# A hybrid decoder layer: the first chunk transposed from raw rows, its 1/rms multiplied into the results, four loads and orders moved

## Chip, core and metric

The kernel runs on one core of a Trainium2 chip. The metric is device time in microseconds (us) of one execution. Engines: TensorE (PE; its weight loads are listed as PEld), VectorE (DVE), ScalarE (ACT), GpSimd (POOL) and SyncE (SP), whose queue issues the DMAs. The kernel before took 1467.82 us, median of three runs (1467.02 to 1468.22).

## What is computed

One layer on x (2048 tokens of 1024), all in float32:

```
hn = rms_norm(x, g_pre);  proj = hn @ w_in            # 1024 -> 4096 columns
rg_x, rg_g, da_q, da_k, da_v, da_g, xa_q, xa_g = split(proj)
A: causal depthwise conv (4) -> RG-LRU scan, times silu(rg_g)
B: (softmax(Q1 K1') - lam softmax(Q2 K2')) V, causal, 4 heads; rms_norm; times silu(da_g)
C: cross attention of 4 heads into rms_norm(mem) @ w_mem_kv (256 tokens), times silu(xa_g)
out = x + rms_norm(concat(A, B, C) @ w_out, g_post)
```

rms_norm(x, g) multiplies each token's row by 1/rms of that row and each column by g. Since 1/rms is one number per token, it may be multiplied before the projection or into its results.

## The kernel before

Every float32 operand is split in a high part (rounded to the matmul's format, on ScalarE) and a low part (the rest, on VectorE or GpSimd); a product is three matmuls, high-high, low-high, high-low (`mm3`, L241).

Tokens go in four chunks of 512, input columns in eight blocks of 128. The projection runs in two passes, chunks 0 and 1, then 2 and 3 (`project`, L847). A pass goes through 16 pairs of column blocks; each pair has four tiles (first and second half for each chunk) of 24 matmuls. Raw weight pieces (128x512) are loaded with three buffers (`w_load`, L321) and converted (`w_conv`, L327), which also issues the load of the piece three further on and later stores the converted piece to DRAM for the second pass. Each finished tile is evicted by a function of its kind: queries and keys, values, gates, cross attention, recurrence (`ev_*`, L472 to L612). Queries, keys, values and gates go through DRAM to the attention.

The order on TensorE is written out by the program: generators (`spawn`, `pump`) yield a time to wait in a modelled clock `now`, which each matmul advances, and the attention's score stream (`s_stream`, L698), its transposes and values (`t_stream`), cross attention and the recurrence's gates (`rg_gates`, L614) are woven between the projection's matmuls so. `room["e"]` counts free buffers for exponentials. The other engines and SP's queue run in order too; their order is made by a scheduler from the program's order, readiness and the priorities in the code.

The head (L370 to L382): one weight piece and the eight half rows of chunk 0 are loaded, tile after tile (a tile is 128 tokens), then weights 1 and 2, chunk 1's rows, and the memory rows. `norm_row` makes 1/rms of a row tile and multiplies its two halves by it in place. `woven` (L384) then transposes the first chunk by TensorE, block by block and two blocks ahead, evicts it with g as scale (`transpose_norm`, L293), and runs the first pair's matmuls for it. The order of the first eight tiles is pair 0 and pair 1 on chunk 0, then both on chunk 1, whose rows are normalised by `norm_steps` (L277) and transposed in the same woven way. Memory's keys and values follow.

At the end of the second pass `load_wout` (L960) loads and converts w_out's rows by groups, and the output projection runs over 16 token tiles.

Of the kernel before, what the change touches and what calls it, by code (L numbers as in the profile page):

```python
# [15 lines left out]
D = 1024  # L16
# [41 lines left out]
def hybrid_layer(  # L58
# [65 lines left out]
    ident = const.tile([128, 128], F32, name="ident")  # L124
    ones_r = const.tile([128, 128], F32R, name="ones_r")
    cmask = const.tile([128, 128], F32, name="cmask")
# [15 lines left out]
    def setup():  # L142

        nc.scalar.preload_act_table_set("natural_log_exp_and_others")
        nc.scalar.dma_start(vec, vecs[:, 0:V_CW])
        make_identity(nc, ident)
        nc.gpsimd.memset(cmask, 0.0)
        nc.gpsimd.affine_select(
            out=cmask, in_=cmask, pattern=[[-1, 128]], compare_op=ALU.is_ge,
            fill=NEG, base=0, channel_multiplier=1)  # L150
        nc.vector.memset(epsb, EPS)
        nc.vector.memset(tinyb, 1e-37)
        nc.vector.tensor_scalar(ones_r, ident, 0.0, 1.0, op0=ALU.mult, op1=ALU.add)

# [108 lines left out]

    def norm_row(row):

        ss = tiny.tile([128, 2], F32, tag="ss1", name="ss1")
        ja, jv = f2("junk", (128, 512)), f2("junk", (128, 512))
        nc.scalar.activation(ja, row[0], AF.Square, accum_out=ss[:, 0:1])
        nc.vector.tensor_tensor_reduce(jv, row[1], row[1], 1.0, 0.0, ALU.mult, ALU.add, ss[:, 1:2])
        r = tiny.tile([128, 1], F32, tag="rs1", name="rs1")  # L270
        with tc.high_priority(offset=2000):
            nc.vector.tensor_add(r, ss[:, 0:1], ss[:, 1:2])
            rsqrt_mean(r, r, D, nc.vector)
            for p in row:
                nc.vector.tensor_scalar_mul(p, p, r)

# [91 lines left out]
    ready = set()  # L368
    stored = set()
    setup()  # L370
    w_load(0)
    xr0 = load_rows(x, 4, "xrow")
    w_load(1, 2)
    xb = bigt("xrows", (128, 4, 2, 512), F32)
    xr1 = [[xb[:, i, j, :] for j in range(2)] for i in range(4)]
    for i in range(4):
        nc.sync.dma_start(xb[:, i].rearrange("p a b -> p (a b)"), x[CH + i * 128:CH + (i + 1) * 128, :])
    mrows = load_rows(mem, 2, "memx")
    w_conv(0)
    for row in xr0:  # L380
        norm_row(row)
    w_conv(1, 2, eng=nc.vector)  # L382

    def woven(c, rows):  # L384

        new_hnT(c)
        os = [ps_m("ip") for _ in range(2)]
        xt = transpose_norm(rows, hnT[c], V_GPRE)
        next(xt)
        next(xt)  # L390
        for kb in range(KB):
            w = wcv[kb // 2]
            for half in range(2):
                cs = slice(half * 128, half * 128 + 128)
                mm3(os[half], w[:, 0, kb % 2, cs], w[:, 1, kb % 2, cs], hnT[c][0][:, kb, :], hnT[c][1][:, kb, :],
                    kb == 0, kb == KB - 1)
            next(xt, None)
            if c == 0:
                if kb in (1, 2, 4, 6):
                    i = {1: 3, 2: 4, 4: 5, 6: 6}[kb]  # L400
                    w_conv(i, eng=nc.vector if i in (3, 5) else nc.gpsimd, pool=pw if i < 6 else p4)
            elif kb % 2:
                w_conv(MEM0 + kb // 2, eng=nc.vector if kb % 4 == 1 else nc.gpsimd)
            pump()
        if c == 0:
            w_conv(7, pool=p4)
        ready.add(c)
        return os

    def prep_mem():  # L410
# [59 lines left out]


    def ev_qk(h, c, which, o):  # L472
        t = f4("qkhl", (128, 2, CH), F32R)
        if which == 0:
            nc.scalar.activation(t[:, 0], o, AF.Copy, scale=DA_SCALE)
            nc.vector.scalar_tensor_tensor(t[:, 1], o, DA_SCALE, asf(t[:, 0]), op0=ALU.mult, op1=ALU.subtract)
        else:
            nc.scalar.copy(t[:, 0], o)
            nc.vector.tensor_sub(t[:, 1], o, asf(t[:, 0]))

        def st():
            for k in range(2):
                rows = asf(t[k * 64:(k + 1) * 64])
                dst = (QD, KD)[which][h][c][k]
                nc.sync.dma_start(dst[0:2].rearrange("l r t -> r l t"), rows)
                if which == 0:
                    nc.sync.dma_start(dst[2], rows[:, 0, :])
        store(st, 3.0)

    def ev_v(hp, c, half, o):  # L490

        t = f4("vhl", (128, 2, 2, 2, 128), F32R)
        ov = o.rearrange("p (t h d) -> p h t d", t=2, h=2)
        for hh in range(2):
            nc.scalar.copy(t[:, 0, hh], ov[:, hh])
            nc.vector.tensor_sub(t[:, 1, hh], ov[:, hh], asf(t[:, 0, hh]))
        def st():
            for hh in range(2):
                nc.sync.dma_start(VD[2 * hp + hh][c][:, :, 2 * half:2 * half + 2, :], asf(t[:, :, hh]))
        store(st, 3.0)  # L500

    def ev_g(hp, c, half, o):
        t = f2("gs", (128, CH))
        sigmoid(t, o)
# [12 lines left out]

    def ev_xa(h, c, which, o):
        if which == 0:
            sg = f2("xag", (128, CH))  # L520
# [62 lines left out]
    def ev_rg(b, c, which, o):  # L583
        if which == 0:
# [5 lines left out]
            else:  # L590
                nc.gpsimd.tensor_copy(xr[:, 0:3], halo[:, b, :])
            nc.scalar.copy(xr[:, 3:515], o)
            if c < NCH - 1:
# [12 lines left out]
            return  # L606
        xc, xh = state.pop("xc")
        gs = f2("rgg", (128, CH))
        sigmoid(gs, o)
# [4 lines left out]
    def rg_gates(b, c, xc, xh, gs):  # L614
        while state["xa_live"]:
            yield 0.5
        if "rgh" not in state:
            rg_weights()
            yield 5.0
        ri = f4("ri", (128, 2, CH))  # L620
        for g in range(2):
            o = ps_s("rgo")
            mm3(o, state["rgh"][:, b, g, :], state["rgl"][:, b, g, :], xh[:, 0], xh[:, 1], True, True)
            with tc.high_priority(offset=PRX):
# [73 lines left out]
    def s_stream(jobs):  # L698

        q2s = {}  # L700

        def q2_load(i):
            if i < 2 * len(jobs) and i not in q2s:
                h, pr = jobs[i // 2]
                if has("qk", h, pr // 4):
                    q2s[i] = load_q2(h, 2 * pr + i % 2)
        due = now[0]
        for ij, (h, pr) in enumerate(jobs):
            while 2 * ij not in q2s:
                q2_load(2 * ij)  # L710
                yield 0.5
            while kready.get((h, pr // 4), 1e9) > now[0]:
                yield 0.5
# [118 lines left out]
    def subln(h, pr, A, B):  # L832
        c, j = divmod(pr, 2)
        s = ps_t("ss", (128, 256))
        mm(s, ones_r, B[:, 0, :], True, False)
        mm(s, ones_r, B[:, 1, :], False, True)
        r = A[:, 1, :]
# [71 lines left out]
    def start_attention():  # L909
        room["e"] = N_E  # L910
        spawn(kv_stream())
# [20 lines left out]
    def prep_next(c):  # L932
        yield from prep_x(c, xn.pop(c), False)
        if c == 2:
            room["e"] += 8
        else:
            room["kv"] += 1
# [20 lines left out]


    def load_wout(grp):  # L960

# [5 lines left out]
        for kb in range(4):  # L967
            raw = f4("woraw")
            nc.sync.dma_start(raw, w_out[4 * grp + kb])
            for j in range(2):  # L970
# [7 lines left out]

    project((2, 3), 80, ORDER_B, {(0, 0): start_b, (15, 2): last_pair})

# [117 lines left out]
```

## Time and profile before

| | |
|---|---|
| median of three runs | 1467.82 us |
| profiled execution | 1467.53 us, its span 1465.7 us |
| TensorE busy | 1412.3 us, 96% of the span |
| VectorE, ScalarE, GpSimd busy | 61%, 53%, 33% |
| mean granted TensorE clock | 0.994 |

The span goes from the first to the last instruction of one profiled execution. Busy time is the union of an engine's instructions; matmuls overlap, so the time from one start to the next is the better measure of one matmul. A wait is the idle time of an engine before an instruction, put down to what released it.

### The profile page before, as it was taken

How to read it: one execution, taken by the hardware profiler on the slowest of the kernel's cores; microseconds unless marked ns; L12 is line 12 of the kernel's file. 1: busy time of each engine (PE TensorE's matmuls, PEld its weight loads, DVE VectorE, ACT ScalarE, POOL GpSimd, SP SyncE). 2: the span in 40 equal slices, each digit the busy share in tenths (PEclk: the TensorE clock that was granted, in tenths of full speed). 3: DMA queues.
4: the chain of work that ended last, by engine and by line, in shares of the span. 5: the costliest groups of instructions: out<-in, count | busy, mean ns of one | idle time of the engine just before them, and what ended most of it. 6: DMA issues, size and time to landing. Idle time of an engine off the chain costs nothing.

```text
span 1465.7 us, 21854 instructions
## 1 busy us (share of the span) xinstructions
PE 1412.3 (96%) x7568; PEld 1199.2 (82%) x7568; DVE 898.3 (61%) x1872; ACT 775.9 (53%) x1900; POOL 477.3 (33%) x568
## 2 busy tenths in 40 slices
PE   5999999999999899999999999999999999999997
PEld 3798889888887678888887898888877888888886
DVE  6531555676644876746547666757678777767222
ACT  6343544666547784745555545555566545554221
POOL 2031333344435632412213222212255333334221
PEclk9999999999999999999999999999999999999999
DMA  8689787745433348356324554232475334322231
GB/s 298 180 263 338 230 240 237 247 143 181 166 119 110 134 163 247 121 173 196 114 97 118 165 177 168 86 113 70 143 251 169 101 135 150 102 76 94 87 122 72
DMA packets 147870, 234.37 MB, mean 160 GB/s; under 512 B 12464, under 2 KB 82224, under 8 KB 147760
## 3 DMA queue, kind: packets, MB, share of 16 engines
q1 hardware_dynamic: 147616, 232.98, 48.8%
q8 instruction: 59, 0.97, 0.3%
q14 instruction: 51, 0.42, 0.1%
q10 hardware_dynamic: 144, 0.01, 0.0%
HBM read 142.76 MB, written 90.18 MB: 159 GB/s over the span
## 4 chain that ended last, share of the span: by engine, by line
PE 73%; DVE 9%; ACT 7%; DMA 4%; POOL 3%; issue 3%; SPq 1%; DVEq 0%; POOLq 0%; ACTq 0%
PE ip L198 36%; PE po L198 16%; PE s L198 7%; PE o L198 6%; PE pt L202 3%; PE xas L198 2%; DVE e L766 1%; DVE nm L740 1%; PE xao L198 1%; DMA q<-QD 1%; DVE xc L600 1%; PE rgo L198 1%; ACT e L742 1%; PE xat L202 1%; POOL e L765 1%
## 5 line engine op out<-in xcount | busy, mean ns | idle before, releaser
L198 PE MATMUL ip<-hnT,wp 128*128 128x512 f32 x2688 | 680.5, 397 | 6.9 <-DVE rgg L610 2.6
L198 PEld LDWEIGHTS ip<-hnT,wp 128*128 128x128 f32 x2688 | 496.0, 190 | 109.8 <-DVE hnT L307 4.5
L742 ACT ACTIVATE e<-s,nm 128x512 f32<-128x512 f32 (+3 forms) x320 | 200.1, 626 | 254.7 <-DVE nm L740 235.8
L740 DVE TENSOR_REDUCE nm<-s 128x1 f32<-128x512 f32 (+3 forms) x320 | 193.4, 605 | 37.4 <-PE s L198 33.1
L198 PE MATMUL po<-wout,yg 128*128 128x512 f32 x768 | 193.4, 393 | 5.0 <-POOL wout L239 2.4
L765 POOL TENSOR_SCALAR e<-e,f 128x512 f32<-128x512 f32 (+3 forms) x160 | 121.3, 773 | 235.5 <-DVE f L761 161.6
L198 PE MATMUL s<-kv,q 128*128 128x512 f32 (+3 forms) x640 | 182.9, 367 | 3.9 <-DMA q<-QD 2.4
L198 PEld LDWEIGHTS po<-wout,yg 128*128 128x128 f32 x768 | 141.1, 188 | 35.4 <-POOL wout L239 4.2
L766 DVE SCALAR_TENSOR_TENSOR e<-e,f 128x512 f32<-128x512 f32 (+3 forms) x160 | 138.0, 887 | 29.9 <-POOL e L765 29.7
L807 DVE TENSOR_TENSOR pthl<-pt,pthl 128x512 fp32r<-128x512 f32 (+1 forms) x144 | 94.5, 656 | 68.0 <-ACT pthl L806 67.5
L198 PE MATMUL o<-pthl,kv 128*128 128x256 f32 (+1 forms) x864 | 134.3, 290 | 1.0 <-DVE pthl L807 0.9
L198 PEld LDWEIGHTS s<-kv,q 128*128 128x128 f32 x640 | 114.5, 189 | 25.1 <-DMA q<-QD 3.0
L239 POOL TENSOR_TENSOR wp<-wraw,wp 128x512 fp32r<-128x512 f32 x67 | 91.1, 1368 | 127.1 <-ACT wp L238 110.8
L198 PEld LDWEIGHTS o<-pthl,kv 128*128 128x128 f32 x864 | 114.1, 189 | 4.5 <-DVE pthl L807 1.8
L806 ACT CAST pthl<-pt 128x512 fp32r<-128x512 f32 (+1 forms) x144 | 80.7, 561 | 55.2 <-PE pt L202 54.5
L239 POOL TENSOR_TENSOR yg<-yraw,yg 128x512 fp32r<-128x512 f32 x48 | 64.2, 1341 | 132.8 <-ACT yg L238 122.4
L198 PE MATMUL ip<-wp,hnT 128*128 128x256 f32 x768 | 99.7, 284 | 1.3 <-POOL wp L239 0.8
L198 PEld LDWEIGHTS ip<-wp,hnT 128*128 128x128 f32 x768 | 95.8, 191 | 3.0 <-POOL wp L239 1.0
L198 PE MATMUL po<-wo,yg 128*128 128x512 f32 x384 | 97.2, 392 | 0.0
L202 PE MATMUL pt<-ident,e 128*128 128x128 f32 x544 | 83.0, 272 | 3.3 <-DVE pthl L807 3.3
L198 PEld LDWEIGHTS po<-wo,yg 128*128 128x128 f32 x384 | 71.0, 188 | 14.3
L202 PEld LDWEIGHTS pt<-ident,e 128*128 128x128 f32 x544 | 66.9, 140 | 18.4 <-DVE pthl L807 3.8
(188 smaller groups left out, 1686.1 us busy)
## 6 DMA issues: line engine op xcount, KB each, us to landing
WD<-wp SPq DMA_DIRECT2D x64, 512.0 KB, 4.7
wp<-WD SPq DMA_DIRECT2D x64, 512.0 KB, 4.3
wraw<-in_w_in_dram SPq DMA_DIRECT2D x64, 256.0 KB, 3.4
q<-QD SPq DMA_DIRECT2D x128, 128.0 KB, 3.7
kv<-KD SPq DMA_DIRECT2D x24, 512.0 KB, 5.9
kv<-VD SPq DMA_DIRECT2D x24, 512.0 KB, 6.2
yraw<-YD SPq DMA_DIRECT2D x48, 256.0 KB, 2.7
QD<-qkhl SPq DMA_DIRECT2D x32, 256.0 KB, 3.5
```

The costliest lines, as they stand in the source:

```text
L198: nc.tensor.matmul(o, w, xx, start=start, stop=stop)
L202: nc.tensor.transpose(o, i, ident)
L239: eng.tensor_sub(lo, raw, asf(hi))
L600: nc.vector.scalar_tensor_tensor(xc[:, 0:CH], xr[:, k:k + CH], vec2[:, cw + k:cw + k + 1], xc[:, 0:CH], op0=ALU.mult, op1=ALU.add)
L740: nc.vector.tensor_reduce(out=nm[:, c, kc:kc + 1], in_=s[:, 0:w], op=ALU.max, axis=AX.X, negate=True)
L742: nc.scalar.activation(e[kc, c][:, 0:w], s[:, 0:w], AF.Exp, bias=nm[:, c, kc:kc + 1], accum_out=l[:, c, kc:kc + 1])
L765: nc.gpsimd.tensor_scalar(e2, e2, f[:, 1, kc:kc + 1], 1.0, op0=ALU.mult, op1=ALU.mult)
L766: nc.vector.scalar_tensor_tensor(e1, e1, f[:, 0, kc:kc + 1], e2, op0=ALU.mult, op1=ALU.add)
L806: nc.scalar.copy(hi[:, 0:n], t[:, 0:n])
L807: nc.vector.tensor_sub(lo[:, 0:n], t[:, 0:n], asf(hi[:, 0:n]))
```

## The change

The first chunk's rows are loaded left halves first, with weights 1 and 2 between and after. They are transposed unnormalised; 1/rms is computed beside the projection (`inv_rms`), laid out along the free axis for all partitions by four TensorE transposes (`spread`, into rB0, which takes one of the twelve buffers for exponentials), and multiplied into the evictions of chunk 0. The second chunk's and memory's loads move into and behind `woven`. The first conversion is by VectorE, the next seven by GpSimd. In `rg_gates` the matmuls that need only the high half come first for both gates. `s_stream` waits until the first query block of a job has been out for 6 us of `now`. The third group of w_out is loaded one tile earlier. The matrix of ones is one column, read as a broadcast.

```diff
-    ones_r = const.tile([128, 128], F32R, name="ones_r")
+    ones_r = const.tile([128, 1], F32R, name="ones_r")
...
+    def inv_rms(tiles, r):
+        n = len(tiles)
+        ss = tiny.tile([128, 2, n], F32, tag="ss0", name="ss0")
+        for j in range(2):
+            for i, row in enumerate(tiles):
+                junk = f2("junk", (128, 512))
+                if i % 2:
+                    nc.vector.tensor_tensor_reduce(junk, row[j], row[j], 1.0, 0.0, ALU.mult, ALU.add,
+                                                   ss[:, j, i:i + 1])
+                else:
+                    nc.scalar.activation(junk, row[j], AF.Square, accum_out=ss[:, j, i:i + 1])
+        nc.vector.tensor_add(r, ss[:, 0], ss[:, 1])
+        rsqrt_mean(r, r, D, nc.vector)
...
     w_load(0)
-    xr0 = load_rows(x, 4, "xrow")
-    w_load(1, 2)
+    xr0 = [[f2("xrow", (128, 512), pool=pe) for _ in range(2)] for _ in range(4)]
+    for j in range(2):
+        for i in range(4):
+            nc.sync.dma_start(xr0[i][j], x[i * 128:(i + 1) * 128, j * 512:(j + 1) * 512])
+        w_load(1 + j)
+    rB0 = f2("rB0", (128, CH), pool=pe)
...
-    for i in range(4):
-        nc.sync.dma_start(xb[:, i].rearrange("p a b -> p (a b)"), x[CH + i * 128:CH + (i + 1) * 128, :])
-    mrows = load_rows(mem, 2, "memx")
-    w_conv(0)
-    for row in xr0:
-        norm_row(row)
-    w_conv(1, 2, eng=nc.vector)
+    mrows = []
+    with tc.high_priority(offset=2000):
+        w_conv(0, eng=nc.vector)
+    w_conv(1, 2)
...
             if c == 0:
+                if kb == 2:
+                    with tc.high_priority(offset=1000):
+                        inv_rms(rows, r0)
+                if kb == 6:
+                    spread(r0, 4, rB0)
+                if kb == 3:
+                    for i in range(4):
+                        t0 = CH + i * 128
+                        nc.sync.dma_start(xb[:, i].rearrange("p a b -> p (a b)"), x[t0:t0 + 128, :])
                 if kb in (1, 2, 4, 6):
...
-                    w_conv(i, eng=nc.vector if i in (3, 5) else nc.gpsimd, pool=pw if i < 6 else p4)
+                    w_conv(i, pool=pw if i < 6 else p4)
...
+            mrows.extend(load_rows(mem, 2, "memx"))
...
+    def spread(r, n, dst):
+        t = ps_t("rb", (128, n * 128))
+        for i in range(n):
+            transpose(t[:, i * 128:(i + 1) * 128], r[:, i:i + 1].to_broadcast([128, 128]))
+        with tc.high_priority(offset=2000):
+            nc.scalar.copy(dst, t)
...
+    def normed_out(o, c):
+        if c:
+            return o
+        n = f2("nrm", (128, CH))
+        nc.vector.tensor_mul(n, o, rB0)
+        return n
+
     def ev_qk(h, c, which, o):
+        o = normed_out(o, c)
...
-            nc.scalar.copy(xr[:, 3:515], o)
+            if c == 0:
+                nc.vector.tensor_mul(xr[:, 3:515], o, rB0)
+            else:
+                nc.scalar.copy(xr[:, 3:515], o)
...
+        os = [ps_s("rgo") for _ in range(2)]
         for g in range(2):
-            o = ps_s("rgo")
-            mm3(o, state["rgh"][:, b, g, :], state["rgl"][:, b, g, :], xh[:, 0], xh[:, 1], True, True)
+            mm(os[g], state["rgh"][:, b, g, :], xh[:, 0], True, False)
+            mm(os[g], state["rgl"][:, b, g, :], xh[:, 0], False, False)
+        for g in range(2):
+            o = os[g]
+            mm(o, state["rgh"][:, b, g, :], xh[:, 1], False, True)
...
+                    landed[i] = now[0] + 6.0
...
-            while kready.get((h, pr // 4), 1e9) > now[0]:
+            while max(kready.get((h, pr // 4), 1e9), landed[2 * ij]) > now[0]:
...
-        room["e"] = N_E
+        room["e"] = N_E - 1
...
-    project((2, 3), 80, ORDER_B, {(0, 0): start_b, (15, 2): last_pair})
+    def last_raw():
+        for kb in range(4):
+            wo_load(2, kb)
+
+    project((2, 3), 80, ORDER_B, {(0, 0): start_b, (15, 2): last_pair, (15, 3): last_raw})
```

`normed_out` is called in the same way by the evictions of gates, cross attention and the recurrence's gates; the values' eviction takes 1/rms, per token there, as the scale of instructions that it has already.

## Rows read from the trace of the kernel before

**Rows 1.** The page's engine shares: busy us (share of the span) and instructions.

```profile
PE 1412.3 (96%) x7568; PEld 1199.2 (82%) x7568; DVE 898.3 (61%) x1872; ACT 775.9 (53%) x1900; POOL 477.3 (33%) x568
```

**Rows 2.** TensorE's waits: who, for whom, us in total, times, longest us.

```profile
PE xt L202 <- DVE xrow L275: 14.3, 4, 9.4
PE rgo L198 <- POOL xchl L604: 4.0, 5, 1.4
PE xas L198 <- DVE xaq L528: 3.4, 3, 1.7
...
PE po L198 <- POOL wout L239: 2.4, 4, 0.7
PE s L198 <- DMA q<-QD: 2.4, 1, 2.4
...
PE po L198 <- ACT wout L238: 1.5, 1, 1.5
```

**Rows 3.** Timeline, head: start us, us, engine, line, operation, tiles, count, idle before.

```profile
3.44 0.62 ACT L238 CAST wp<-wraw 128x512 fp32r<-128x512 f32 x1 [1.43 <-DMA wraw<-in_w_in_dram]
...
6.74 2.31 SPq L377 DMA_DIRECT2D xrows<-in_x_dram  x4
...
6.93 0.16 DVE L272 TENSOR_TENSOR rs<-ss 128x1 f32<-128x1 f32 x1
...
8.58 0.16 DVE L256 TENSOR_TENSOR rs<-rs,rst 128x1 f32<-128x1 f32 x1
...
9.67 0.63 ACT L268 ACTIVATE junk<-xrow 128x512 f32<-128x512 f32 x1 [0.56 <-DMA xrow<-in_x_dram]
...
11.30 1.12 ACT L238 CAST wp<-wraw 128x512 fp32r<-128x512 f32 x2
...
16.20 0.69 ACT L306 ACTIVATE hnT<-xt,vec 128x512 fp32r<-128x512 f32 x1 [1.26 <-PE xt L202]
...
16.95 2.93 PE L198 MATMUL ip<-hnT,wp 128*128 128x512 f32 x6
...
30.98 0.48 DVE L291 TENSOR_SCALAR xrows<-xrows,rs 128x512 f32<-128x512 f32 x1
```

**Rows 4.** Chain of waits, first 120 us: start us, us, what (x count).

```profile
2.60 4.77 DMA xrow<-in_x_dram
...
50.49 0.44 PE xt L202 x4
50.92 1.38 PE ip L198 x6
```

**Rows 5.** Timeline of TensorE, the last stalls of the first chunk.

```profile
34.15 1.19 PE L198 MATMUL ip<-hnT,wp 128*128 128x512 f32 x4 [1.38 <-DVE hnT L307]
36.06 11.18 PE L198 MATMUL ip<-hnT,wp 128*128 128x512 f32 x48 [0.72 <-DVE qkhl L476]
```

**Rows 6.** Projection results, 100 to 450 us: min/median/max ns, first and last start.

```profile
L505 DVE TENSOR_TENSOR gs<-ip,gs x8: 681/692/694, 133.2 to 274.7; 128x512 f32<-128x512 f32 x8
```

**Rows 7.** Timeline, a conversion on GpSimd and one on VectorE.

```profile
26.21 1.42 POOL L239 TENSOR_TENSOR wp<-wraw,wp 128x512 fp32r<-128x512 f32 x1 [3.02 <-ACT wp L238]
...
26.67 1.50 DVE L239 TENSOR_TENSOR wp<-wraw,wp 128x512 fp32r<-128x512 f32 x1 [0.20 <-ACT wp L238]
```

**Rows 8.** Windows: us, busy of PE, PEld, DVE, ACT, POOL; clock, DMA share, GB/s.

```profile
9.40:17.00 7.60, 2.70 (x9) 1.50 (x9) 6.64 (x31) 5.13 (x15) 0.00 (x0) 1.00 1.04 409
200.00:400.00 200.00, 196.44 (x1154) 171.78 (x1153) 132.67 (x311) 118.38 (x312) 80.61 (x103) 1.00 0.61 201
```

**Rows 9.** Timeline of TensorE, behind a wait of the gate projections.

```profile
482.06 4.15 PE L198 MATMUL ip<-hnT,wp 128*128 128x512 f32 x12
```

**Rows 10.** Chain of waits, two pieces that end in a TensorE wait.

```profile
136.71 8.90 DMA q<-QD
...
1083.92 7.74 DMA woraw<-in_w_out_dram
```

**Rows 11.** The sums' weight loads: min/median/max ns, first and last start.

```profile
L198 PEld LDWEIGHTS ss<-sq,ones_r x64: 187/188/192, 172.1 to 1385.6; 128*128 128x128 f32 x64
```

More of the change, by code (lines that the diff above doesn't have):

```diff
@@ L152, in setup @@
         nc.vector.memset(tinyb, 1e-37)
-        nc.vector.tensor_scalar(ones_r, ident, 0.0, 1.0, op0=ALU.mult, op1=ALU.add)
+        nc.vector.tensor_scalar(ones_r, ident[:, 0:1], 0.0, 1.0, op0=ALU.mult, op1=ALU.add)
     def setup2():
@@ L262, in sigmoid @@
         nc.scalar.activation(o, o, AF.Exp, scale=-1.0)
[L264 to L275, printed above, removed]
+    def inv_rms(tiles, r):
[11 more added lines that the diff above has]
+        rsqrt_mean(r, r, D, nc.vector)
     def norm_steps(tiles, gap, eng=nc.gpsimd, prio=2000):
@@ L369, in hybrid_layer @@
     stored = set()
+    r0 = const.tile([128, 4], F32, name="r0")
     setup()
     w_load(0)
-    xr0 = load_rows(x, 4, "xrow")
-    w_load(1, 2)
+    xr0 = [[f2("xrow", (128, 512), pool=pe) for _ in range(2)] for _ in range(4)]
[4 more added lines that the diff above has]
+    rB0 = f2("rB0", (128, CH), pool=pe)
     xb = bigt("xrows", (128, 4, 2, 512), F32)
     xr1 = [[xb[:, i, j, :] for j in range(2)] for i in range(4)]
-    for i in range(4):
-        nc.sync.dma_start(xb[:, i].rearrange("p a b -> p (a b)"), x[CH + i * 128:CH + (i + 1) * 128, :])
-    mrows = load_rows(mem, 2, "memx")
-    w_conv(0)
-    for row in xr0:
-        norm_row(row)
-    w_conv(1, 2, eng=nc.vector)
+    mrows = []
+    with tc.high_priority(offset=2000):
+        w_conv(0, eng=nc.vector)
+    w_conv(1, 2)
     def woven(c, rows):
@@ L493, in ev_v @@
         ov = o.rearrange("p (t h d) -> p h t d", t=2, h=2)
-        for hh in range(2):
-            nc.scalar.copy(t[:, 0, hh], ov[:, hh])
-            nc.vector.tensor_sub(t[:, 1, hh], ov[:, hh], asf(t[:, 0, hh]))
+        for i in range(2):
+            if c:
+                hi, lo, oi = t[:, 0, i], t[:, 1, i], ov[:, i]
+                nc.scalar.copy(hi, oi)
+                nc.vector.tensor_sub(lo, oi, asf(hi))
+            else:
+                hi, lo, oi = t[:, 0, :, i], t[:, 1, :, i], ov[:, :, i]
+                r = r0[:, 2 * half + i:2 * half + i + 1]
+                nc.scalar.activation(hi, oi, AF.Copy, scale=r)
+                nc.vector.scalar_tensor_tensor(lo, oi, r, asf(hi), op0=ALU.mult, op1=ALU.subtract)
         def st():
@@ L502, in ev_g @@
     def ev_g(hp, c, half, o):
+        o = normed_out(o, c)
         t = f2("gs", (128, CH))
@@ L518, in ev_xa @@
     def ev_xa(h, c, which, o):
+        o = normed_out(o, c)
         if which == 0:
@@ L591, in ev_rg @@
                 nc.gpsimd.tensor_copy(xr[:, 0:3], halo[:, b, :])
-            nc.scalar.copy(xr[:, 3:515], o)
+            if c == 0:
+                nc.vector.tensor_mul(xr[:, 3:515], o, rB0)
+            else:
+                nc.scalar.copy(xr[:, 3:515], o)
             if c < NCH - 1:
@@ L607, in ev_rg @@
         xc, xh = state.pop("xc")
+        o = normed_out(o, c)
         gs = f2("rgg", (128, CH))
@@ L698, in s_stream @@
     def s_stream(jobs):
-        q2s = {}
+        q2s, landed = {}, {}
         def q2_load(i):
@@ L834, in subln @@
         s = ps_t("ss", (128, 256))
-        mm(s, ones_r, B[:, 0, :], True, False)
-        mm(s, ones_r, B[:, 1, :], False, True)
+        ones = ones_r.to_broadcast([128, 128])
+        mm(s, ones, B[:, 0, :], True, False)
+        mm(s, ones, B[:, 1, :], False, True)
         r = A[:, 1, :]
@@ L934, in prep_next @@
         if c == 2:
-            room["e"] += 8
+            room["e"] += 9
         else:
@@ L957, in y_granule, with wo_load @@
         return g
+    woraw = {}
+    def wo_load(grp, kb):
+        if (grp, kb) not in woraw:
+            raw = woraw[grp, kb] = f4("woraw", pool=pw if grp == 2 and kb == 3 else p4)
+            nc.sync.dma_start(raw, w_out[4 * grp + kb])
+        return woraw[grp, kb]
     def load_wout(grp):
@@ L967, in load_wout @@
         for kb in range(4):
-            raw = f4("woraw")
-            nc.sync.dma_start(raw, w_out[4 * grp + kb])
+            raw = wo_load(grp, kb)
             for j in range(2):
```

## The prediction

> **What bounds the kernel now.** I read the engine shares first: TensorE is busy for 1412.3 of 1465.7 us, no other engine above 61% [rows 1]. Time can only be won where TensorE stands still or runs slow, so the list of TensorE's waits comes next [rows 2]. One place holds a third of them: 14.3 us before the transposes of the first rows of x. The change also aims at the gate projections (4.0 us, five waits for the low halves that GpSimd makes), the start of the output projection (2.4 and 1.5 us) and one query block (2.4 us). The timeline of the head shows why it is long: a row tile needs both halves loaded, its square sum, 1/rms and two multiplies before it can be transposed, four tiles one after the other, and the first projection matmul comes at 16.95 us [rows 3]. The profiled run took 1467.53 us, 1.8 more than its span and 0.3 under the median of 1467.82; I sum against 1467.5.
>
> **The change part by part.**
>
> *Start of the first chunk.* Eight loads of x stood behind one weight piece; the fourth landed at 7.37 us [rows 4]. After the change the fourth is the last of the left halves, so all four tiles are complete for input blocks 0 to 3 at that time, with as many bytes ahead of it as before. To it I add the transposes (four take 0.44) [rows 4], the ScalarE eviction (0.69) [rows 3] and 0.1 of hand-over: first projection matmul at 8.6 us instead of 16.95, 8.35 us sooner. Its weight piece is long there (cast at 3.44). Weights 1 and 2 were cast from 11.30 on [rows 3] as ninth and tenth load behind the first weight; weight 1 is now the fifth, so earlier, and wanted at about 14. Weight 2 keeps its place, and the right halves of x, now ahead of it, have landed by 11.3 too; input block 4, which needs them, is transposed at about 16. No load is late.
>
> *Rest of the first chunk.* From 16.95 us to the next tile's first matmul at 36.06 [rows 5] are 19.1 us. The work in it: six matmuls at the slow start, 2.93 us, 0.49 each [rows 3]; six groups of four transposes at 0.44 and seven groups of six matmuls at 1.38, 0.23 each [rows 4]: 2.93 + 2.64 + 9.66 = 15.2. So 3.9 us were stalls, 1.38 and 0.72 of them with names [rows 5]. The slow six I charge again. The change adds one group of four transposes, the spread of 1/rms (0.44), and takes out eight row multiplies. The 0.72 ended with the VectorE subtraction that follows ScalarE's copy of the accumulator; now one VectorE multiply frees it, 0.69 [rows 6], which fits beside the last three matmuls of the other half, so 0.1 is left. That needs 1/rms: the right halves' square sums start by 11.3, two per engine at 0.63 and a short read [rows 3], done by 13.5; the chain from one tile's sum to its 1/rms took from 6.93 to 8.74 [rows 3]; r is there at about 16, the spread comes at 22. For the other stalls I take half of what they were, 1.7 (bounds 0 and 5). 15.2 + 0.4 + 1.7 + 0.1 = 17.4: the next tile starts at 26.0 instead of 36.06, 10.0 us gained.
>
> *Moves in the head.* The second chunk's loads go behind weight loads on SP's queue that wait for a free buffer, memory's behind the whole first chunk. The second chunk is close: its last multiply ended at 31.46, 24.7 us after its first load was issued at 6.74 [rows 3]. If the loads are issued only where they now stand, at about 17, it is ready at 41.7; the next tile's 48 matmuls take 11.2 [rows 5], so the transposes want it at 37.2. That is a wait of 4.5 at worst, and none if the loads slip ahead of the waiting weights. I take 0.8. Memory's rows are wanted later still. Net for the head: 9.2 (5 to 11.8, the latter without any stall).
>
> *Conversions from VectorE to GpSimd.* Weights 1 to 7 now go to GpSimd, at some 1.4 each 10 us in the 16 of the chunk. The trace shows the two engines in each other's way: a VectorE conversion beside one on GpSimd that began 0.46 earlier ended 0.54 after it, having taken 1.50 [rows 7], over twice a VectorE multiply of that size. VectorE has four square sums there and eight multiplies of the second chunk; at 0.8 each that is 9.6 us at most, and TensorE sees it only where a low-half eviction stands behind, as in the 1.38 wait. This is within the 1.7 and its bound of 5.
>
> The Trainium skill (SBUF — State Buffer, Who interferes with whom) has a rule that speaks against this move: a VectorE instruction with two SBUF inputs and a GpSimd instruction share a port pair, and the later one waits for the whole of the other. The 1.50 agrees. By the rule alone the new multiplies, which read one operand from PSUM, stay out of it, and the bound of the twelve instructions is the same 9.6.
>
> *1/rms multiplied into the results.* 24 evictions of chunk 0 (8 of queries and keys, 4 gates, 8 of cross attention, 4 of the recurrence's gates) get a multiply of 0.69 [rows 6], 16.6 us of VectorE; four ScalarE copies become VectorE multiplies; for the values the scale goes into instructions that are there. VectorE was busy for 132.7 of 200 us in that stretch [rows 8]. TensorE's accumulators come free sooner (one step of 0.69 instead of a copy and a subtraction); what comes later is the chain behind them, above all the cross-attention scores, and whatever queues on VectorE behind a multiply: score maxima, low halves of the probabilities. Bounds: a gain of 24 x 0.1, if the sooner release counts, and a loss of all 16.6. I take a loss of 1.5, near the lower end: the list has three waits, 3.4 us, on the low halves of cross attention's queries in all sixteen tiles [rows 2].
>
> *Gate projections.* The second gate's two matmuls on the high half go ahead of the wait for GpSimd: 2 x 0.23 = 0.46 us of cover at each of five waits, some shorter than that. Gain 2.2 (0 to 4.0). The slow stretch behind one such wait, twelve matmuls in 4.15 us instead of 2.8 [rows 9], I leave as it is; if it goes too, it is 1.4 more.
>
> *w_out.* The waits there, 3.9 us in all [rows 2], begin with a load on the chain, 7.74 us from 1083.92 [rows 10]. Issued a tile earlier, it is 5.5 us sooner (24 matmuls at 0.23, more with the attention between them), which is more than the 3.9 of waits; its conversions remain, but begin sooner. Gain 3.5. Against it: four loads, 2.1 MB at 409 GB/s [rows 8], stand ahead of values and queries on SP's queue, put them back by 5.1 us, and hold buffers that evictions use. Bounds: 3.9 gained; 1.6 lost, if 5.1 take the place of the 3.5.
>
> *Query loads.* The new condition holds a job back until its first block's query has been out for 6 us. The one stall of that kind ended a load of 8.90 us issued at 136.71 [rows 10], which is that of the first job's second block: it is issued while the first block is worked on, and the condition does not reach it. 0 (gain at most 2.4, loss 1). One slot of twelve less for exponentials: 0, as the rest of the stream keeps its pace (loss 1 at most, by the same wait). Ones read through a broadcast: 64 weight loads of 188 ns [rows 11], beside matmuls; 0, and 12 lost if each took twice as long and nothing covered it.
>
> Sum: -9.2 + 1.5 - 2.2 - 3.5 = -13.4; 1467.5 - 13.4 = 1454.
>
> **The rivals.** *The head fills up elsewhere.* ScalarE has some 20 us of work for the 16 of the chunk (8 evictions at 0.69, 7 casts at 0.62, 12 square sums of both chunks at 0.8), 2.5 more than the stalls I allow, and the second chunk is late by 4.5, 3.7 more than I allow: 1460. For it: these durations. Against: the second chunk's square sums have time until 37. *More than counted:* no stall in the head (2.6 more), the waits at the gates gone with their slow stretch (3.2 more): 1448. *The change does not do what it says:* ScalarE or the queue holds the transposes until the right halves are in, at 11.3 instead of 7.4: 3.9 less, 1458. *w_out's loads push back the values:* 1.6 instead of -3.5, 1459. *Slower:* the multiplies of chunk 0 end up on the path between projection and attention. VectorE works in order, so each stands before maxima and exponentials; if TensorE sees all 24 and every fourth brings a slow stretch of 1.4, it is 16.6 + 8.4 - 1.5 = 23.5 more, 1477. With half of that it is 1466, no change; it decides from some 16 multiplies on the path. Against it: a third of VectorE's time there is free.
>
> **How the numbers follow.** Forecast 0.55, own range 1450 to 1459; full head 0.15; more 0.10; late start 0.04; w_out 0.04; half of the multiplies seen 0.05; all of them 0.07. Range 1445 to 1464: the low end adds the query's 2.4 and a little to the case of more; the high end is the head at 5 with nothing else but the evictions' 1.5. It leaves out the last two cases. What a measurement of this kernel can tell is 0.2%, 2.9 us: faster 0.88, within it 0.05, slower 0.07.
>
> **What would show it.** First projection matmul near 8.6 us, second tile near 26, the second chunk's transposes near 37 without a wait for its multiplies; waits on the gates' low halves shrunk by about 0.46 each; no wait for w_out at the start of the output projection; the query wait still there. I am wrong if the second tile starts after 30, if cross-attention's waits grow beyond 5 us, or if the head's gain is gone by 450 us.

## The result, and the profile after

The changed kernel took 1480.3 us (median of four runs, 1479.4 to 1481.6) against 1468.0 beside it: 1.0077 of before, interval [1.0060, 1.0095]. The forecast was 1454, faster. The profiled execution took 1479.63 us, its span 1477.8. Measured again in a later group of runs the change gave 1.0053 (after_again, below).

TensorE's share first, then its waits (who, for whom, us in total, times, longest), both of the changed kernel:

```profile
PE 1418.5 (96%) x7572; PEld 1203.9 (81%) x7572; DVE 901.1 (61%) x1871; ACT 774.2 (52%) x1891; POOL 479.4 (32%) x571
```

```profile
PE xt L202 <- DMA xrow<-in_x_dram: 6.2, 4, 4.2
PE ip L198 <- DVE rgg L658: 5.7, 2, 3.3
PE xas L198 <- DVE xaq L572: 4.5, 5, 1.7
PE s L198 <- DMA q<-QD: 4.1, 1, 4.1
PE o L198 <- DVE pthl L860: 4.1, 5, 1.9
PE rgo L198 <- DVE xchl L650: 3.9, 3, 2.3
PE xt L202 <- DVE hnT L309: 3.6, 2, 1.9
PE s L198 <- ACT e L795: 2.9, 2, 2.0
PE rgo L198 <- POOL xchl L651: 2.7, 3, 1.5
PE kv L198 <- DVE wp L239: 2.6, 1, 2.6
...
PE xt L202 <- DVE xrows L293: 1.9, 2, 1.4
```

Beside [rows 2]: the 14.3 us before the first transposes are 6.2, the output projection's waits for w_out are gone, the gates' waits for the low halves fell from 4.0 to 2.7. In their place stand waits that VectorE ends: accumulators (rgg), the recurrence's high halves (xchl), chunk 2's transposes (hnT). The query's wait grew from 2.4 to 4.1.

A list of waits doesn't say where a gain is lost. For that I count the projections' matmuls (names ip, kv, po) in both traces and subtract the start times of the same one. Negative is earlier than before, in us; the experiments' names are explained below.

| place (time in before) | after | u_rg | u_mul | kv_late | head_only | cured | before_gates | wo_alone |
|---|---|---|---|---|---|---|---|---|
| first projection matmul (16.9) | -6.6 | -6.4 | -5.6 | -5.5 | -6.5 | -6.0 | -0.4 | -0.1 |
| second tile (36.1) | -8.0 | -8.2 | -6.5 | -7.3 | -7.7 | -7.6 | -0.3 | 0.8 |
| past chunk 1's transposes (63.6) | -5.5 | -5.7 | -6.3 | -4.9 | -7.5 | -5.2 | -0.3 | 0.8 |
| in memory's keys and values (93.8) | -0.6 | -1.0 | -1.3 | -0.1 | -2.4 | -3.1 | -0.4 | 0.8 |
| ahead of the query block (136.5) | -0.9 | -2.0 | -2.7 | -1.1 | -3.7 | -4.1 | 2.4 | 2.5 |
| past the query block (152.9) | 0.6 | -0.3 | -1.2 | -5.7 | -7.9 | -8.6 | 0.5 | 1.6 |
| 284.1 | 0.5 | -0.7 | -1.2 | -6.0 | -7.9 | -9.0 | 0.6 | 1.6 |
| past cross attention (448.6) | 4.1 | 2.8 | 0.1 | -2.0 | -6.7 | -5.5 | 0.6 | 1.6 |
| past the recurrence (556.2) | 15.7 | 8.5 | 4.3 | 9.4 | -5.0 | 0.6 | 4.4 | 3.1 |
| ahead of the output projection (1083.1) | 15.2 | 7.3 | 3.6 | 9.1 | -5.7 | 0.2 | 6.0 | 3.9 |
| in it (1125.7) | 12.2 | 6.0 | 0.6 | 6.1 | -8.7 | -2.7 | 6.1 | 1.0 |
| last matmul (1457.8) | 12.1 | 6.3 | 1.4 | 6.1 | -8.4 | -3.1 | 6.4 | 0.9 |

The first column has four stories: a head that wins 8.0 us; its loss by 153 us (2.5 at chunk 1's transposes, 4.9 in memory's keys and values, 1.5 at the query block); 15 us lost from 284 to 556 us; 3 us won at the output projection. What ended each is in the timelines. The head (TensorE; start, duration, tiles, count, idle before and its releaser):

```profile
14.13 2.85 PE L198 MATMUL ip<-hnT,wp 128*128 128x512 f32 x6
...
28.11 2.12 PE L198 MATMUL ip<-hnT,wp 128*128 128x512 f32 x8 [0.16 <-DVE nrm L502]
```

From 14 us on no stall is longer than 0.16 us. The stretch from the first projection matmul to the second tile took 17.8 us where 17.4 were forecast, but this agreement is luck: most of the 1.7 us that I had left for stalls went into a second slow group of six matmuls (2.85 us; those that follow take 1.64). Memory's keys and values, VectorE and then TensorE:

```profile
78.41 0.28 DVE L162 TENSOR_TENSOR lam_s<-lam_in 128x128 f32<-128x128 f32 x1
...
82.80 1.21 DVE L179 TENSOR_TENSOR sp<-sp 128x4 f32<-128x4 f32 x1
84.04 0.17 DVE L180 TENSOR_SCALAR sp<-sp 128x4 f32<-128x4 f32 x1
84.24 0.16 DVE L179 TENSOR_TENSOR sp<-sp 128x4 f32<-128x4 f32 x1
84.44 1.14 DVE L180 TENSOR_SCALAR sp<-sp 128x4 f32<-128x4 f32 x1
...
86.89 0.68 DVE L239 TENSOR_TENSOR wp<-wraw,wp 128x512 fp32r<-128x512 f32 x1
```

```profile
87.62 8.52 PE L198 MATMUL kv<-wp,memT 128*128 128x256 f32 x54 [2.61 <-DVE wp L239]
```

`setup2` (constants of the attention and the recurrence) is some 30 short VectorE instructions. Before, its two loads were issued at 58.4 and 61.4 us and it ran from 63.5 to 70.7, ahead of memory's keys and values. Now the loads stand behind waiting weight loads on SP's queue (73.2 and 74.2) and it runs in the middle of that stage; the weight conversion at 86.89 is queued behind it (ScalarE had done its part by 84.2), and TensorE waits 2.61 us and then runs at a mean granted clock of 0.72 from 88 to 94 us (1.00 in that stretch before).

### The profile page after: what moved, and what is told of

It is laid out like the page before. It is cut to its first block, busy times and chain, and to the rows that moved or that the text cites. A ratio compares the mean times of both kernels' runs of the same rounds, so it can differ in the third digit from the quotient of the medians.

```text
span 1477.8 us, 21854 instructions
## 1 busy us (share of the span) xinstructions
PE 1418.5 (96%) x7572; PEld 1203.9 (81%) x7572; DVE 901.1 (61%) x1871; ACT 774.2 (52%) x1891; POOL 479.4 (32%) x571
## 4 chain that ended last, share of the span: by engine, by line
PE 57%; DVE 9%; ACT 6%; issue 5%; POOL 4%; DMA 1%; SPq 0%; DVEq 0%; POOLq 0%; ACTq 0%
PE ip L198 24%; PE po L198 16%; PE s L198 6%; PE o L198 5%; PE pt L202 3%; DVE nm L793 2%; PE xas L198 1%; PE xao L198 1%; ACT e L795 1%; DVE e L819 1%; POOL wp L239 1%; DVE xc L647 1%; POOL e L818 1%; PE xat L202 1%; DVE pthl L860 1%
## 5 line engine op out<-in xcount | busy, mean ns | idle before, releaser
L239 POOL TENSOR_TENSOR wp<-wraw,wp 128x512 fp32r<-128x512 f32 x70 | 94.4, 1359 | 124.0 <-ACT wp L238 123.6
L198 PEld LDWEIGHTS po<-wo,yg 128*128 128x128 f32 x384 | 71.0, 188 | 14.3
```

The lines of the kernel that those rows point to most:

```text
L198: nc.tensor.matmul(o, w, xx, start=start, stop=stop)
L239: eng.tensor_sub(lo, raw, asf(hi))
```

## The experiments

They ran in four groups on three chips, each group beside runs of the kernel before, which spread from 1467 to 1477 us; so ratios are compared (the change again and kv_late are from one chip, rg_kv and those built on it from another). A profile is one execution; where it and the median disagree, I say so.

| run | edit | median us | ratio to before, interval |
|---|---|---|---|
| after_again | the change | 1479.8 | 1.0053 [1.0034, 1.0072] |
| u_rg | change, old gate order | 1477.1 | 1.0029 [1.0017, 1.0042] |
| u_mul | change, no multiplications | 1469.9 | 0.9986 [0.9972, 1.0000] |
| u_set38 | change, setup2 earlier | 1480.6 | 1.0054 [1.0037, 1.0071] |
| u_wo | change, w_out as before | 1480.7 | 1.0054 [1.0037, 1.0071] |
| setup_late | change, setup2 at the attention | 1482.7 | 1.0068 [1.0044, 1.0091] |
| rec_plain | change, no multiplications in the recurrence | 1474.1 | 1.0011 [0.9998, 1.0024] |
| before_gates | before, new gate order | 1474.3 | 1.0017 [1.0000, 1.0033] |
| rec_on_pool | change, old gate order, recurrence's multiplications on GpSimd | 1482.2 | 1.0067 [1.0042, 1.0091] |
| kv_late | change, head 1's keys and values later | 1475.0 | 1.0024 [1.0013, 1.0036] |
| wo_alone | before, w_out earlier | 1469.0 | 0.9987 [0.9974, 0.9999] |
| wo_kv | before, w_out earlier, head 1's keys and values later | 1465.9 | 0.9962 [0.9951, 0.9972] |
| rg_kv | kv_late, old gate order | 1469.5 | 0.9983 [0.9969, 0.9997] |
| head_only | rg_kv, no multiplications | 1460.0 | 0.9930 [0.9908, 0.9951] |
| cured | rg_kv, setup2's loads earlier | 1465.9 | 0.9966 [0.9952, 0.9980] |
| cured_rows | cured, chunk 1's rows earlier | 1465.7 | 0.9958 [0.9943, 0.9973] |

**One part undone at a time.** In u_rg the loop of `rg_gates` is that of before; in u_mul `normed_out` returns its argument and values and recurrence are evicted as for the other chunks; in u_set38 `store(setup2, 52.0)` is `38.0`; in u_wo the hook `(15, 3): last_raw` is out.

> The changed kernel (1480.3) with the gate projections in the old order of matmuls. Theory 1 (three separate places: 5 us in the memory stage, some 11 us around the recurrence from 450 to 560 us, half of them by the new order, which lets the gates' sigmoids start later): 1475, the waits of the projection on the gate eviction (5.7 us) back to 3. Theory 2 (the multiplications by 1/rms on VectorE cost the time, wherever they stand): 1480 to 1482. Theory 3 (the new order alone spoils the recurrence): 1470 or less.

> The changed kernel with the multiplications of chunk 0's results left out (the results of chunk 0 stay unnormalised; 1/rms and its spread are still computed). Theory 1: the cross attention's 3 us and half of the recurrence's 11 come back, 1472. Theory 2: 1464 to 1468, as 24 multiplications of 0.69 are 16.6 us. Theory 3: 1478 to 1480.

> The changed kernel with the small set-up chain of the recurrence's constants (some 25 VectorE instructions of 0.16 us and two small loads) issued at 38 instead of 52 of the modelled clock, so before the memory stage. Theory 1: the wait of memory's keys on VectorE's weight conversion at 87.6 us (2.6) and the slow clock behind it go, 5 us of the head's gain stay, 1475.5. Theories 2 and 3: 1480, as the weights of that stage are limited by their loads and the place of the chain does not matter.

> The changed kernel without the early load of w_out's third group. Theory 1, and my prediction's step: the waits at the start of the output projection come back, 1484 to 1485. Rival: what the early load gains is given back by attention's values behind it, 1481 to 1482.

The old gate order brings back 5.9 us of the 11.6 lost in the recurrence (8.5 - 2.8 against 15.7 - 4.1 in the table), leaving out the multiplications 7.4 there and 2.3 in cross attention. That fits theory 1, separate places, though the multiplications weigh more there than it said. u_set38 won nothing, and not for the reason of theories 2 and 3: its VectorE instructions came so early that they waited 4.7 us for their loads, and memory's transposes with them. u_wo lost 5.0 us at the start of the output projection and got 2.6 back behind it; that it was 2.9 ahead until then comes from steps of 1.3 and 1.6 us in the recurrence, and two executions of the change differ there by 1.5. Its median doesn't resolve the part.

**The place of setup2, once more.** All of `setup2` goes to the start of the attention, at a lower priority.

> The changed kernel with setup2 (two small loads, some 25 short VectorE instructions) moved behind memory's keys and values, to where attention starts. The changed kernel gave 1.0077 of before. Theory 1, the data of the second query block set a floor: the 2.6 us wait for a weight conversion near 88 us and the slow clock behind it go, TensorE comes 4 to 5 us earlier to 140 us, but the query block still lands at 145 to 147 us, the wait for it grows from 4.1 to 8 or 9 us, and the end stays within 2 us of the changed kernel: 1.006 to 1.008. Theory 2, what is saved there is kept: the query wait stays near 4 us and the end comes 4.5 us sooner: 1.0045.

Neither, though the ratio lies where theory 1 had it: the wait in memory's stage went (4.7 us won there), but the constants' load was issued only at 133.4 us, into full DMA engines (mean busy share 1.00 to 1.04 from 130 to 142 us), and landed 8.6 us later. VectorE stood still for it (VectorE, then TensorE's first wait):

```profile
141.97 0.29 DVE L162 TENSOR_TENSOR lam_s<-lam_in 128x128 f32<-128x128 f32 x1 [19.32 <-DMA lam_in<-in_lams_dram]
142.18 0.68 DVE L501 TENSOR_TENSOR nrm<-ip,rB 128x512 f32<-128x512 f32 x1
```

```profile
PE ip L198 <- DVE nrm L501: 11.3, 2, 11.1
```

The experiment missed its aim, and shows what a short instruction costs that waits in order: 11 us of TensorE, through the multiplication behind it that frees an accumulator.

**The floor at the query block.** In `kv_stream`, ahead of head 1:

```diff
+            if h == 1:
+                yield 45.0
```

> The changed kernel once more, beside the runs that it is compared with here. 1.004 to 1.0077 of before; in the trace the wait for the second query block is 3.5 to 4.5 us and ends at 145 to 147 us.

> The changed kernel with the first loads of head 1's keys and values issued 45 us later, behind the second query block instead of ahead of it. Theory 1, the bytes ahead of the query block set the time at which TensorE gets past 146 us, whatever the head gained: four loads of 0.5 MB less are some 5 us of transfer, so the block lands 3 to 4 us sooner, the wait falls from 4.1 to under 1.5 us, and the end comes 2.5 to 4 us sooner than in the changed kernel. Theory 2, weights and the copies that go to DRAM fill the queues all the same: the block still lands after 145 us, the wait stays above 3 us, and the end does not move.

The change came as expected (1.0053, a wait of 3.6 us that ended at 146.5). kv_late took theory 1, and a little more of it: 0.29% or 4.3 us less than the change by the ratios. TensorE around 146 us, before, of the change and of kv_late:

```profile
140.99 2.28 PE L198 MATMUL ip<-hnT,wp 128*128 128x512 f32 x9
145.65 0.81 PE L198 MATMUL s<-kv,q 128*128 128x256 f32 x2 [2.38 <-DMA q<-QD]
```

```profile
140.13 2.29 PE L198 MATMUL ip<-hnT,wp 128*128 128x512 f32 x9
146.53 0.98 PE L198 MATMUL s<-kv,q 128*128 128x256 f32 x2 [4.11 <-DMA q<-QD]
```

```profile
139.88 2.29 PE L198 MATMUL ip<-hnT,wp 128*128 128x512 f32 x9
142.01 0.40 PE L198 MATMUL s<-kv,q 128*128 128x256 f32 x2
```

The change comes there 0.9 us sooner than before and goes on 0.9 later. kv_late comes when the change does and doesn't wait, and behind it is 5.7 us ahead of before where the change is 0.6 behind. Only 1.1 of these 5.7 come from the head (row 136.5 of the table). The other 4.6 are a wait and a slow stretch that the kernel before has as well: the mean granted clock from 145 to 150 us is 0.68 before, 0.66 in the change and 1.00 in kv_late. In the change the DMA engines' mean busy share is 1.00 from 110 to 120, 0.82 from 120 to 130, 0.97 from 130 to 140 and 1.04 from 140 to 147 us; before it was much the same. In the change's variants without this edit TensorE came to that place between 140.5 (u_mul) and 146.0 us (u_set38), and went on between 144.6 and 147.3: of 5.5 us half (2.7) was left. So the transfer is a partial floor: what comes sooner to it waits longer, but not by the whole.

**Gate order and multiplications apart.** before_gates puts the new loop into the kernel before; rec_plain takes `normed_out` and the new `xr` multiplication out of `ev_rg` alone; rec_on_pool has the old loop and, for chunk 0, this:

```diff
-                nc.vector.tensor_mul(xr[:, 3:515], o, rB0)
+                nc.scalar.copy(xr[:, 3:515], o)
+                nc.gpsimd.tensor_mul(xr[:, 3:515], xr[:, 3:515], rB0)
```

(and the same two steps for the gate).

> The kernel before with the new order of the gate matmuls alone. Theory 1, the order only moves the pause: the wait for the low half shrinks by some 0.5 to 0.9 us at each place, but the next accumulator is freed by a VectorE multiply that comes no sooner, so the wait before the next projection matmul grows by as much (3.3 us instead of 1.25 near 487 us), and a longer single pause brings a slow stretch: 1 to 6 us longer, 1.0007 to 1.004. Theory 2, the order is a gain by itself and cost time only beside the multiplications of chunk 0: 1 to 2.2 us shorter, 0.9985 to 0.9993.

> The changed kernel with the multiplications of chunk 0 by 1/rms left out in the recurrence alone (four inputs, evicted by ScalarE again, and four gates): its results there are not normalised. The new order of the gate matmuls stays. Theory 1, the multiplications stand in VectorE's queue between convolution, scan and low halves: of the 11.5 us that the stage from 453 to 572 us lost, 6 to 7.5 come back, as they did with all multiplications left out; 1.003. Theory 2, they are cheap there and those of cross attention are what costs: under 3 us come back; 1.006.

> The changed kernel with the old order of the gate matmuls, and with the recurrence's multiplications of chunk 0 by GpSimd behind a ScalarE copy instead of by VectorE. The old order alone gave 1.0029, with 5.6 us lost against before in the stage from 453 to 565 us. Theory 1, it was VectorE's queue: the loss in that stage falls to under 2 us; 1.0005. Theory 2, it is the length of the chain (0.57 for the copy and 1.3 on GpSimd instead of 0.69): the loss stays at 5.6 us or grows; 1.003 to 1.005.

The kernel before near 480 us (TensorE, then VectorE; [rows 9] stands between the first two lines), and then before_gates, TensorE and VectorE at the same place:

```profile
480.67 0.73 PE L198 MATMUL rgo<-xchl,rgh 128*128 128x512 f32 x2 [1.40 <-POOL xchl L604]
...
487.45 2.79 PE L198 MATMUL ip<-hnT,wp 128*128 128x512 f32 x11 [1.25 <-DVE rgg L610]
```

```profile
486.73 0.67 DVE L610 TENSOR_TENSOR rgg<-ip,rgg 128x512 f32<-128x512 f32 x1
```

```profile
480.58 0.50 PE L198 MATMUL rgo<-xchl,rgh 128*128 128x512 f32 x1
...
482.71 0.73 PE L198 MATMUL rgo<-xchl,rgh 128*128 128x512 f32 x2 [0.93 <-POOL xchl L604]
483.27 2.88 PE L198 MATMUL ip<-hnT,wp 128*128 128x512 f32 x12
489.48 6.89 PE L198 MATMUL ip<-hnT,wp 128*128 128x512 f32 x29 [3.32 <-DVE rgg L610]
```

```profile
481.46 7.36 DVE L291 TENSOR_SCALAR xrow<-xrow,rs 128x512 f32<-128x512 f32 x8 [0.94 <-POOL rs L256]
488.75 0.67 DVE L610 TENSOR_TENSOR rgg<-ip,rgg 128x512 f32<-128x512 f32 x1
```

The order does what it promised: 0.93 instead of 1.40 of wait, and the twelve matmuls behind take 2.88 instead of the 4.15 of [rows 9]. And none of it is kept, since the next tile needs an accumulator that the multiplication of rgg frees, and this stands behind eight row multiplications of chunk 2. It starts 8.17 us after the first gate matmul here (488.75 - 480.58) and started 8.19 after it before (486.73 - 478.54). Two short pauses (1.40 and 1.25) became a shorter and a long one (0.93 and 3.32). What the clock does behind them varies: before, its mean from 483 to 489 us was 0.86; in before_gates it stayed at 1.00 from 489 to 500 and was 0.83 from 500 to 510; in the change, behind a wait of 3.29 us at this place, it is 0.80 from 492 to 507. Theory 1: 0.17% or 2.5 us by the ratio, with an interval that begins at no change, and 6.4 us in the profiled execution.

rec_plain took theory 1 too, and a little more of it: by the same count of matmuls the recurrence's stage lost 3.8 us instead of 11.6. The order alone costs that stage 3.8 us (before_gates) and the multiplications alone 5.7 (u_rg); together they cost 11.6, more than the sum. rec_on_pool took theory 2, the loss growing to 12.2: there the longest wait for the high halves grew to 5.2 us at once (waits of that stage, 455 to 580 us):

```profile
PE rgo L198 <- DVE xchl L651: 9.1, 3, 5.2
PE rgo L198 <- POOL xchl L652: 4.2, 5, 1.1
```

So unloading VectorE is not enough; the chain from accumulator to high half counts, and who stands in it. VectorE before, then in the change:

```profile
488.66 2.33 DVE L600 SCALAR_TENSOR_TENSOR xc<-xr,vec,xc 128x512 f32<-128x512 f32 x3
491.09 0.43 DVE L603 CAST xchl<-xc 128x512 fp32r<-128x512 f32 x1
```

```profile
491.47 0.68 DVE L658 TENSOR_TENSOR rgg<-ip,rgg 128x512 f32<-128x512 f32 x1
492.07 0.41 DVE L685 TENSOR_SCALAR ri<-ri 128x512 f32<-128x512 f32 x1
492.40 0.68 DVE L637 TENSOR_TENSOR xr<-ip,rB 128x512 f32<-128x512 f32 x1
493.19 0.55 DVE L644 TENSOR_SCALAR xc<-xr,vec 128x512 f32<-128x512 f32 x1
493.77 0.75 DVE L647 SCALAR_TENSOR_TENSOR xc<-xr,vec,xc 128x512 f32<-128x512 f32 x1
496.99 1.23 DVE L689 TENSOR_TENSOR_SCAN ri<-rga,ri 128x512 f32<-128x512 f32 x1 [2.47 <-POOL ri L688]
498.13 0.73 DVE L647 SCALAR_TENSOR_TENSOR xc<-xr,vec,xc 128x512 f32<-128x512 f32 x1
500.80 0.69 DVE L502 TENSOR_TENSOR nrm<-ip,rB 128x512 f32<-128x512 f32 x1 [1.94 <-PE ip L198]
501.40 0.74 DVE L647 SCALAR_TENSOR_TENSOR xc<-xr,vec,xc 128x512 f32<-128x512 f32 x1
502.06 3.26 DVE L293 TENSOR_SCALAR xrows<-xrows,rs 128x512 f32<-128x512 f32 x8
505.23 0.42 DVE L650 CAST xchl<-xc 128x512 fp32r<-128x512 f32 x1
```

Before, ScalarE copied the input (487.42), VectorE went through the convolution in one piece and cast its result at 491.09; TensorE took it at 495.74 without a wait. In the change xr waits for VectorE's turn, the scan (waiting 2.47 for GpSimd) and nrm (waiting 1.94 for TensorE) have got in between the convolution's four steps, then eight row multiplications; the cast ends at 505.65 and TensorE has waited 2.30. The multiplications' own 0.68 us each are a small part of it. That the order of the queue, and not the added time, makes most of the loss is read from this one place; no run changed VectorE's order alone.

**What the parts are worth without each other's losses.** rg_kv is kv_late with the old loop; head_only is rg_kv without multiplications; cured splits `setup2` (loads by `store(load2, 30.0)`, the rest by `store(setup2, 50.0)`); cured_rows issues chunk 1's rows at `kb == 2` instead of 3.

> The changed kernel with two edits: the old order of the gate matmuls, and head 1's first keys and values issued 45 us later. The second alone gave 1.0024. Theory 1, the two losses add: the old order brings back 5 to 7 us in the stage from 450 to 570 us also here; 0.998 to 0.9995. Theory 2, the order cost its time only where TensorE came later to that stage, or the same pause shows elsewhere: under 2 us come back; 1.001 to 1.0025.

> The same kernel (old gate order, late keys and values of head 1) with the multiplications of chunk 0 by 1/rms left out everywhere: its results are not normalised, and what is left of the change is the start of the first chunk and w_out's loads. Theory 1, the multiplications cost 8 to 11 us also with the old gate order: 0.991 to 0.993. Theory 2, most of their price came from the gate order beside them: under 4 us; 0.996 or more.

> The changed kernel with the old gate order, the late keys and values of head 1, and setup2's two small loads issued earlier, near 50 us, ahead of weight loads that wait for buffers, so that its VectorE instructions run before memory's keys and values. Theory 1, with the query's wait gone nothing holds back what is saved before it: the 4.7 us lost near 88 us arrive at the end; 3 to 4.7 us shorter than with the first two edits alone. Theory 2, the query block is again what comes last near 146 us: under 1.5 us.

> The kernel with the three edits, and chunk 1's rows issued one input block sooner, ahead of one more weight load. Theory 1, the rows land some 2 us sooner, the waits of 1.4 and 0.5 us before their transposes near 48 us go, and 1.5 to 2.5 us of it arrive at the end. Theory 2, the weight behind them, or their square sums beside the first chunk, wait instead: no change, or up to 2 us longer.

rg_kv: 0.41% under kv_late, theory 1 by the ratios; 4.8 us come back in the recurrence's stage (its profiled execution, 1473.0 us, was the slowest of its ten and shows under 1 us at the end). head_only: 9.5 us under rg_kv by the medians on the same chip, 7.8 by the ratios, theory 1; of 13.9 in the profiled executions 4.1 lie by 64 us, 4.3 in cross attention, 4.9 in the recurrence. cured: 3.5 us under rg_kv by the medians and 2.5 by the ratios, with intervals that overlap. In the trace it is 4.4 ahead past the query block, but 1.8 of that it already had at 64 us; memory's stage cost it 2.1 instead of 4.9. So the wait of that stage was setup2's (it is gone), and the size stays between the theories. cured_rows: no change, theory 2; its transposes wait 1.71 us near 49 as in cured.

**w_out, and a better version.**

> The kernel before with the earlier loads of w_out's third group alone. Theory 1, the wait at the start of the output projection goes as it did in the changed kernel, where 4.7 us came back near 1110 us, and nothing is given back: 4 to 5 us shorter, 0.9965 to 0.9975. Theory 2, the loads push back values and queries, and another wait takes its place: within 1.5 us of before, 0.999 to 1.001.

> The kernel before with two edits: the earlier loads of w_out's third group, and the first loads of head 1's keys and values issued 45 us later. If both waits go: 4.5 and 2 us shorter, 0.9955. If the query's wait stays: 0.997. If the late keys and values make head 1 wait for them: 0.998 or more.

wo_alone won 4.7 us at the start of the output projection and gave 1.8 back behind it, where the attention's last values wait 1.9 us for VectorE's low halves (pthl): 2.9 in the trace, 0.13% (1.9 us) by the ratio, between the two theories. In wo_kv the query's wait is gone, but its trace (the slowest of its ten executions) has a wait of 3.3 us for a weight's high part ahead of that place, so how much each edit gives stays open. wo_kv is 0.38% faster than before, cured_rows 0.42%: both beat both kernels, and can't be told apart. The first does it with two small edits.

## Why the prediction was wrong

The forecast was 13.4 us faster; the trace ends 12.1 slower. Of these 25.5 us, 15.8 lie between 153 and 556 us, where I had summed +1.5 and -2.2 and 15.1 were lost; 6.1 lie between 64 and 153 us, where I had nothing; 3.7 lie in the head. So the steps that failed most are those on the multiplications and the gates, then the one on the moved loads. By the prediction's own steps:

*Start of the first chunk, rest of it, moves.* Right in mechanism, less in size: first projection matmul at 10.35 instead of 8.6, since TensorE waited 1.44 us for ScalarE's eviction, which stood behind a weight's cast and a square sum (8.31 and 9.00 us); second tile at 28.1 instead of 26.0. For chunk 1's rows I took 0.8 of a worst 4.5; the waits are 1.9, the loss 2.5. 8.0 - 2.5 = 5.5 us ahead at 58 us where I had 9.2 in the sum.

*"Memory's rows are wanted later still."* I looked at the rows alone. The step moved everything behind them on SP's queue as well, and with `setup2`'s loads some 30 VectorE instructions went into the one stage where weights are converted just in time: 4.9 us, the largest loss of the head's gain and no term of the sum. cured, where they are moved back, loses 2.1 in that stage and ends 2.5 to 3.5 us sooner than rg_kv.

*Query loads, "0".* I asked what the new condition does to that wait, and not what the wait does to a gain. It took the last 0.9 us of the head and 0.6 more. A wait that ends with a transfer through full DMA engines takes back part of whatever was won ahead of it, here about half over the variants; how much of the head's 8.0 it would have held, had they come so far, no run shows. In my own rows stood a block under way for 8.90 us [rows 10], and a stretch at 409 GB/s to measure it by [rows 8]. The rival *head fills up elsewhere* named chunk 1's rows, and neither of the other two places. One slot less for exponentials, and the new condition itself, were not tested apart. The ones read through a broadcast cost nothing, as forecast: their 64 weight loads take 187 to 192 ns as in [rows 11].

*1/rms multiplied into the results, +1.5.* Measured at 7.8 to 9.5 (head_only against rg_kv, ratios and medians), within the bounds I gave (-2.4 to 16.6), and far from the end that I took. I chose it because one row list had short waits in cross attention, and read "a third of VectorE's time is free" as room. Room over 200 us is no answer to where in an in-order queue an instruction stands. The slower rival named this mechanism and came to 1477, within 4 us of the result; I gave it 0.07 and against it that same third. That it came so near is luck: it charged the multiplications 25 us and kept the whole gain of the head.

*Gate projections, -2.2.* Wrong in sign: 0.17% longer alone, 0.24% (u_rg against the change again) to 0.41% (rg_kv against kv_late) with the multiplications. I priced the cover at each wait, which came as said (1.40 became 0.93), and not what is late next; the row for it (the wait for rgg behind [rows 9]) I had not taken up.

*w_out, -3.5.* Right at the wait, 4.7; net it is 2.9 in the trace and 1.9 by the ratio.

Of the signs that I had named, the query's wait and w_out came as said, and the second tile came before 30 us. Cross attention's waits stayed under 5 us (4.5), though its stage lost 3.6: a limit on one list of waits misses what is lost elsewhere in the stage. The head's gain was gone by 450 us, indeed all but 0.6 us of it by 94.

## What to carry to other kernels

Before a gain at the start of a kernel is counted, look for the next wait that a transfer ends and ask whether that transfer would come sooner too; if the DMA engines are full ahead of it, part of the gain ends there (here about half). An instruction added to an in-order engine is priced by what stands before and behind it at that place, a wait that is cut by what is late next; average load tells neither. A moved load moves the whole queue behind it: list those instructions as well.

## What the runs showed of the hardware

A VectorE instruction on four elements per partition, 0.16 us by itself, took 1.21 and 1.14 us beside GpSimd's conversions, and each ended 0.03 us after the conversion beside it (VectorE's stand above, at 82.80 and 84.44). Eight row multiplications took 7.33 us beside GpSimd's instructions at 484 us and 3.26 at 502 without them. GpSimd's two conversions, then VectorE at 484 us, of the change:

```profile
82.69 1.29 POOL L239 TENSOR_TENSOR wp<-wraw,wp 128x512 fp32r<-128x512 f32 x1 [5.09 <-ACT wp L238]
84.26 1.29 POOL L239 TENSOR_TENSOR wp<-wraw,wp 128x512 fp32r<-128x512 f32 x1 [0.28 <-ACT wp L238]
```

```profile
484.22 7.33 DVE L293 TENSOR_SCALAR xrow<-xrow,rs 128x512 f32<-128x512 f32 x8 [0.94 <-POOL rs L256]
```

The Trainium skill (SBUF — State Buffer, Who interferes with whom) says that the blocked engine waits for the whole instruction of the other, and counts one-input VectorE operations in their two-port modes among those that contend; the trace agrees, with the 0.03 us and with 7.33 against 3.26 us. The same load of `setup2`'s constants took 3.1 us when issued at 62.6 us (u_set38) and 8.6 us when issued at 133.4 in the full stretch (setup_late).
